# The gate product beside the sum of squares, latent norms behind counted products, and another order in the last dilated pair

## The chip, the cores and the metric

One core of a Trainium2 chip runs the whole program in one launch. The metric is the device time of one execution in microseconds (us). The kernel before took 2313.22 us, the median of three runs (2310.89 to 2314.72).

## The reference, cut to what matters

Two decoder layers over 512 positions and a model width of 1024, all in float32. Each layer is a feed-forward half step, a token mixer and a second feed-forward half step; the mixer is latent attention (MLA) in layer 0 and dilated attention in layer 1. Each of these six sub-layers sits in the same sandwich:

```python
def sandwich(x, fn, pre_g, post_g, shift, scale, gate, res_w):
    hn = rmsnorm(x, pre_g) * (1 + scale) + shift
    y = rmsnorm(fn(hn), post_g)
    return x + res_w * gate * y

def mla(h, ...):                      # the start
    lat = h @ w_in
    cq, ckv, k_rope = lat[..., :384], lat[..., 384:640], lat[..., 640:]
    q  = rmsnorm(cq,  q_norm)  @ w_q_up
    kv = rmsnorm(ckv, kv_norm) @ w_kv_up

def dilated_attention(h, ...):        # 16 heads, groups of dilation 1, 4 and 16
    o_g, lse_g = windowed attention of each group, lse_g its log of the sum of exponentials
    alpha = softmax over g of lse_g
    return (sum over g of alpha_g * o_g) @ w_o
```

## The kernel before, in words

Activations lie transposed in SBUF for the products: eight chunks `k` of 128 model columns by 512 positions, each split into a rounded part `hh` and a remainder `hl`. A float32 product is three matmuls (`mm3`, L120-126, rows L124, L125 and L126 of the trace): hi by hi, hi by lo, lo by hi. Weights come by DMA on SyncE's queue (SP) as 512 KB tiles `raw`; ScalarE (ACT) rounds them (`whi`, L107) and VectorE (DVE) forms the remainder in two halves (`wlo`, L109).

**Order of the work.** A tile scheduler orders each engine's instructions by priority. Inside `manual_schedule` an engine listed there keeps the order in which the code is written. `after(n, step)` puts off a step until `count` has seen `n` more matmul units; `mm3` counts two units for 512 columns and one for 256.

**A transition** (L390-410) goes from one sub-layer to the next. For each of four tiles of 128 positions, `tail` finishes the output product; `y_part` (L376 adds, L378 copies) brings its two halves from PSUM to SBUF, `y_done` squares them on ACT with the row sum, `scale_of` (L291 on DVE, L292 a power on GpSimd, POOL) makes the reciprocal root, `tile_done` (L413, L414) scales by root and gate and adds to the residual `x`, and `normal` (L308) makes the next normalised input. After two tiles `turn` (L418-434) transposes the pair chunk by chunk on TensorE (PE), and `modulate` applies scale and shift: for most chunks DVE makes `u` (L279), ACT rounds it to `hh` (L280) and DVE subtracts for `hl` (L281); for the chunks in `SPARE` ACT makes `hh` and `u` (L275, L276) and POOL subtracts (L277). The first products (`head`) of the next sub-layer then run over the chunks as they come. At the start of the program the same `modulate` follows a fold of the modulation weights (L158, two custom DVE instructions, each with an accumulator read, for the shift and two for the scale).

**MLA's start.** After the latents are projected, `norm` (L654-667) sums squares with narrow products (`sums`, L225), takes the root on POOL (`root`, L240 and L242), spreads it over the partitions with four products (`spread`, L248) and scales the latents, all in one call.

**The last dilated pair.** The 16 heads go in eight pairs. `scores` forms the logits, `exps` (L1058) their exponentials, `norm` (L1069-1085) the reciprocal of their sum, which goes to memory and back to change its layout (`x4` from `z0`, `d0`, then `r`), `turn` transposes the exponentials, `weigh` (L1132) multiplies them with the values, and `mix(p, step)` alternates turn and weigh. At the end `weigh` multiplies by `r` (L1142) and `put_o` hands the result to the output product. For the last pair, PE alone is ordered by hand: six `part` calls of the output product (three of its eight column blocks), then the mixes with two parts between. `part` takes one of four `mm` banks of PSUM, and the bank is free once L378 has copied it out. The last column block of `tail` needs the last pair's output.

Of the kernel before, what the change touches and what calls it, by code (L numbers as in the profile page):

```python
# [7 lines left out]
F32 = mybir.dt.float32  # L8
# [6 lines left out]
P = 128  # L15
# [14 lines left out]
SB = 4  # L30
HOT = 400
HEAD = 3
SPARE = (2, 3, 6, 7)
TURN = 26
START = 4
HT = SEQ // 2
# [16 lines left out]
class Trunk:  # L53
# [79 lines left out]
    def count(self, n):  # L133
        for d in self.due:
            d[0] -= n
        while self.due and self.due[0][0] <= 0:
            self.due.pop(0)[1]()

    def mod(self, l, n, k):
        nc = self.nc  # L140
# [169 lines left out]
    def start(self, sub):  # L310
        nc = self.nc
        mods = [(sub.l, 3 * sub.i + n) for n in (0, 1)]
        raws = {}

        def fetch(k):
            for m in mods:
                raws[m, k] = self.mod_load(*m, k)

        def fold(k):
            for m in mods:  # L320
                self.mod_halves(*m, k, raws.pop((m, k)))

        def feed(us, ks):
            for u in us:
                sub.gate_up_mm(u, 0, SEQ, banks[u], ks)

        self.first = sub
        fetch(0)
        xt = [self.bank("mm" if k < 4 else "aux") for k in range(KT)]
        with self.tc.manual_schedule(engines={ACT, DVE}):  # L330
            for i in range(TT):
                t, ss, x = [self.s(), self.s()], self.pair(), self.halves(i)
                for d in range(2):
                    self.square(x[d], t[d], ss[:, d : d + 1])
                r = self.scale_of(ss)
                for d in range(2):
                    nc.vector.tensor_scalar(t[d], x[d], r, None, ALU.mult)
                for k in range(KT):
                    nc.tensor.transpose(
                        xt[k][:, i * P : (i + 1) * P], t[k // 4][:, k % 4 * P :][:, :P], self.ident  # L340
                    )
            nc.scalar.activation(self.cs, self.cs, AF.Silu)
        self.new_h()
        units, ks = [], []
        banks = {}
        for kind, n in sorted([(n, 1) for n in range(START)] + [(n, 0) for n in range(KT)]):
            kind, n = n, kind
            if kind:
                sub.gate_up_load(n, n >= SLOTS // 2)
                banks[n] = [self.bank("mm" if 2 * n + g < 4 else "aux") for g in range(2)]  # L350
                units.append(n)
                feed((n,), ks)
                continue
            if n:
                fetch(n)
            fold(n)
            self.modulate(sub, n, 0, SEQ, xt[n], n in (3, 5, 7))
            ks.append(n)
            feed(units, (n,))
            if n == 0:  # L360
                for k in range(1, KT):
                    src, xt[k] = xt[k], self.s()
                    nc.scalar.activation(xt[k], src, AF.Copy)
        for u in units:
            sub.gate_up_out(u, 0, SEQ, banks[u])
# [16 lines left out]
    def y_done(self, i, d):  # L382
        with self.tc.high_priority(offset=HOT):
            if d == 0:
                self.ss = self.pair()
            self.square(self.y[i][d], self.t("sq", SB), self.ss[:, d : d + 1])

    def transition(self, sub, nxt):
        for u in (sub, nxt):
            if u:  # L390
                self.settle(u)
        if nxt:
            self.new_h()
        for i in range(TT):
            sub.tail(i)
            self.tile_done(nxt, i)
            if nxt and i % 2:
                self.after(TURN, lambda i=i: self.turn(nxt, i - 1))
            if nxt and i == 1:
                nxt.prepare()  # L400
        if nxt:
            for lo in (0, HT):
                for u in range(nxt.heads):
                    nxt.head(u, lo, lo + HT)
        self.count(4 * TURN)

    def tile_done(self, nxt, i):

        nc = self.nc
        r = self.scale_of(self.ss)  # L410
        for d in range(2):
            y, c = self.y[i][d], slice(d * SEQ, (d + 1) * SEQ)
            nc.vector.scalar_tensor_tensor(y, y, r, self.gb[:, c], ALU.mult, ALU.mult)  # L413
            nc.vector.tensor_tensor(self.x[:, i, c], self.x[:, i, c], y, ALU.add)  # L414
            if not nxt:
                nc.sync.dma_start(self.a["out"][i][:, c], self.x[:, i, c])
        if nxt:
            self.normal(i, self.y[i])  # L418

# [15 lines left out]

class Ffn:
    heads = HEAD

    def __init__(self, t, l, i):
        self.t, self.l, self.i, self.s = t, l, i, 0 if i == 0 else 1  # L440
# [172 lines left out]

class Mla(Mixer):
    heads = 6
    busy = False
    w_o = "mla_o"

# [35 lines left out]
    def norm(self, us, at, lo, hi):  # L654
        t, nc = self.t, self.t.nc
        n = hi - lo
        rb = t.rms([self.sq[u, lo] for u in us], n, P * len(us))
        for j, u in enumerate(us):
            if lo == 0:
                self.latn[u] = [t.s(F32R) for _ in range(2)]  # L660
            hh, hl = [x[:, lo:hi] for x in self.latn[u]]
            v = t.t("u", UB)[:, :n]
            nc.vector.scalar_tensor_tensor(
                v, self.lat[u][:, lo:hi], t.glat[:, at + j : at + j + 1], rb, ALU.mult, ALU.mult
            )
            nc.scalar.activation(hh, v, AF.Copy)
            nc.vector.tensor_tensor(hl, v, f(hh), ALU.subtract)

    def project(self, w, at, us):
        t = self.t  # L670
# [38 lines left out]
    def rope(self, g):  # L709
# [15 lines left out]


    BESIDE = {
        0: (("key", 0, 1),),
        1: (("query", 0, 1),),
        2: (("value", 2, 0),),  # L730
        3: (("value", 3, 0),),
# [92 lines left out]
    def rest(self):  # L824
        self.t.gates(self)
        self.wv, self.wqk, self.v, self.q, self.k = [], {}, {}, {}, {}
        pipe = Pipe(2)
        self.key(0, 0)
        self.rope(0)
        self.query(0, 0)  # L830
        self.value(0, 0)
        self.value(1, 0)
        for c in range(8):
            for i in range(4):
                if (c, i) == (7, 0):
                    self.t.new_y()
                self.attend(c, i, pipe)
                for name, *args in self.BESIDE.get(4 * c + i, ()):
                    getattr(self, name)(*args)
        for ns in ((3, 4, 5), (6, 7)):  # L840
            pipe.step()
            for n in ns:
                self.part(n)
        pipe.flush()


class Dil(Mixer):
    heads = 6
    busy = True
    w_o = "dil_o"  # L850
    BLOCKS = (
# [196 lines left out]
    def exps(self, p):  # L1048
        nc = self.t.nc
        pair = self.pairs[p]  # L1050
        for u, (g, blocks) in enumerate(self.BLOCKS):
            for e in range(2):
                y = pair["y"][u, e]
                at = 0
                for i, k0, n, b0 in blocks:
                    c = y[:, at : at + n]
                    one = slice(e, e + 1)
                    nc.scalar.activation(  # L1058
                        c,
                        c,  # L1060
                        AF.Exp,
                        bias=pair["top"][:, g, i, one],
                        scale=-1.0,
                        accum_out=pair["z"][:, g, i, one],
                    )
                    at += n
        self.norm(pair)

    def norm(self, pair):  # L1069
        t, nc = self.t, self.t.nc  # L1070
        z = pair["z"]
        z0 = t.dram.tile([2, SEQ, 2], F32, tag="z0", name="z0", bufs=2)
        d0 = t.dram.tile([2, SEQ], F32, tag="d0", name="d0", bufs=2)
        self.natural(z0, z)
        x = t.tmp.tile([P, 2, 4, 2], F32, tag="x4", name="x4", bufs=2)
        nc.sync.dma_start(x, z0.rearrange("g (p r) v -> p g r v", r=4))
        d = t.tmp.tile([P, 2, 4], F32, tag="w4", name="w4", bufs=2)
        dr = d.rearrange("p e r -> p r e")
        nc.vector.tensor_tensor(dr, x[:, 0], x[:, 1], ALU.add)
# [31 lines left out]
                nc.vector.tensor_copy(x[:, :n], b[:, :n])  # L1111
            out.append(x)

    def weigh(self, p, step):
        t, nc = self.t, self.t.nc
        g, _, _, products = self.TURNS[step]
        pair = self.pairs[p]
        if step == 0:
            pair["acc"] = t.bank("aux")
        v = self.qkv[p, 3 * g + 2]  # L1120
        for nth, (kt, c0, n, at) in enumerate(products):
            for e in range(2):
# [6 lines left out]
                else:  # L1129
# [3 lines left out]
                    out,  # L1133
                    v[:, kt * P + 64 * e :][:, :64],
                    rhs,
                    start=step == nth == 0,
                    stop=step == nth == 3,
                    skip_group_check=True,
                )
        if step == 3:  # L1140
            x = t.s()
            nc.vector.tensor_tensor(x, pair["acc"], pair["r"], ALU.mult)  # L1142
            self.of.append(x)
# [7 lines left out]
    def rest(self):  # L1151
# [30 lines left out]
        for x in self.of[PART:]:  # L1182
            self.put_o(x)
        self.exps(7)
        with t.tc.manual_schedule(engines={PE}):
            for n in range(6):
                self.part(n)
            for step in range(5):
                self.mix(7, step)
                if step in (1, 2):  # L1190
                    self.part(5 + step)
        self.put_o(self.of[-1])


# [113 lines left out]
```

## Time and profile before

| | |
|---|---|
| Time, median of three runs | 2313.22 us |
| The profiled execution: its own time, its span | 2314.05 us, 2312.3 us |
| Mean granted TensorE clock | 0.99 |
| PE busy | 2247.3 us, 97% of the span |
| DVE busy | 1191.8 us, 52% |
| ACT busy | 870.6 us, 38% |
| POOL busy | 121.4 us, 5% |

The span is the time from the first to the last recorded event; 1.75 us of the execution lie around it. Matmuls are pipelined, so a record of 0.39 us for a matmul of 512 columns can start 0.23 us after the one before. An idle time in brackets behind a row is the engine's own, just ahead of that row, with the instruction that ended it. The granted clock is a share of full speed (1.00 is 2.4 GHz, 0.50 is 1.2 GHz).

### The profile page before, as it was taken

To read this page: it belongs to the slowest core of one execution; us is meant where nothing else is said; L and a number is where in the kernel's file an instruction comes from. 1 tells how busy PE (TensorE), PEld (TensorE's weight loads), DVE (VectorE), ACT (ScalarE), POOL (GpSimd) and SP (SyncE) were. 2 spreads that over 40 slices of the span, in tenths; PEclk is the share of its full clock that TensorE was granted. 3 is DMA by queue.
4 is the path that set the end of the run, shared out by engine and by line. 5 is a ranking of instruction groups with operands and counts; after the bars stand their busy time and mean duration, and the time that the engine had idled before them with its cause. 6 is when DMAs were issued, how large, how long until landed. Compare 5 with 4: busy or idle time off the path is not lost. (4 is left out here: it accounts for less than half of the span.)

```text
span 2312.3 us, 30176 instructions
## 1 busy us (share of the span) xinstructions
PE 2247.3 (97%) x11418; PEld 1857.3 (80%) x11418; DVE 1191.8 (52%) x2674; ACT 870.6 (38%) x1773; POOL 121.4 (5%) x163
## 2 busy tenths in 40 slices
PE   7999999999999999999999999999999979999998
PEld 5888888877788888888888888778778758888887
DVE  7666576576655456464555453344434356233344
ACT  4422235577533222352222352443433435232232
POOL 0000001210110000020000020000000002000000
PEclk9999999999999999999999999999999989999999
DMA  8675573111345365244654423333333312242230
GB/s 311 171 241 183 171 237 104 52 56 46 105 141 182 97 205 183 81 146 124 194 171 149 123 81 100 86 86 88 94 85 83 93 38 95 74 128 91 82 110 37
DMA packets 119925, 284.55 MB, mean 123 GB/s; under 512 B 43985, under 2 KB 48356, under 8 KB 119780
## 3 DMA queue, kind: packets, MB, share of 16 engines
q1 hardware_dynamic: 119780, 282.63, 40.0%
q8 instruction: 89, 1.46, 0.3%
q14 instruction: 56, 0.46, 0.1%
HBM read 280.19 MB, written 2.39 MB: 122 GB/s over the span
## 5 line engine op out<-in xcount | busy, mean ns | idle before, releaser
L124 PE MATMUL mm<-s,whi 128*128 128x512 f32 (+1 forms) x2132 | 804.7, 379 | 10.2 <-ACT s L280 7.0
L125 PE MATMUL mm<-s,whi 128*128 128x512 f32 (+1 forms) x2132 | 800.2, 375 | 0.9 <-POOL s L277 0.7
L126 PE MATMUL mm<-s,wlo 128*128 128x512 f32 (+1 forms) x2132 | 799.1, 375 | 0.0
L107 ACT ACTIVATE whi<-raw 128x1024 fp32r<-128x1024 f32 (+1 forms) x356 | 370.2, 1053 | 989.8 <-PE mm L125 447.8
L109 DVE TENSOR_TENSOR wlo<-raw,whi 128x512 fp32r<-128x512 f32 (+1 forms) x712 | 464.9, 692 | 414.2 <-ACT whi L107 409.2
L124 PEld LDWEIGHTS mm<-s,whi 128*128 128x128 f32 x2132 | 403.6, 190 | 92.7 <-ACT s L280 8.2
L125 PEld LDWEIGHTS mm<-s,whi 128*128 128x128 f32 x2132 | 403.9, 189 | 71.7 <-POOL s L277 2.1
L126 PEld LDWEIGHTS mm<-s,wlo 128*128 128x128 f32 x2132 | 403.8, 189 | 71.2
L124 PE MATMUL mm<-whi,s 128*128 128x512 f32 x848 | 333.4, 393 | 17.1 <-DVE s L378 16.4
L125 PE MATMUL mm<-wlo,s 128*128 128x512 f32 x848 | 331.1, 390 | 0.0
L126 PE MATMUL mm<-whi,s 128*128 128x512 f32 x848 | 330.9, 390 | 0.0
L143 DVE CUSTOM_DVE_ANT_0 raw<-raw,cs 128x1024 f32<-128x1024 f32 x128 | 158.0, 1238 | 115.7 <-DMA raw<-w_mod 115.3
L124 PEld LDWEIGHTS mm<-whi,s 128*128 128x128 f32 x848 | 159.8, 188 | 52.5 <-DVE s L378 16.9
L126 PEld LDWEIGHTS mm<-whi,s 128*128 128x128 f32 x848 | 159.6, 188 | 33.5 <-issue 0.2
L125 PEld LDWEIGHTS mm<-wlo,s 128*128 128x128 f32 x848 | 159.9, 189 | 32.9 <-issue 0.2
L483 DVE TENSOR_TENSOR gg<-silu,mm 128x512 f32<-128x512 f32 (+1 forms) x95 | 60.3, 636 | 172.4 <-PE mm L126 172.0
L376 DVE TENSOR_TENSOR s<-mm,s 128x512 f32<-128x512 f32 x112 | 76.7, 689 | 126.2 <-PE mm L126 126.1
L292 POOL TENSOR_TENSOR mv<-mv,mhalf 128x1 f32<-128x1 f32 x48 | 27.3, 568 | 1492.6 <-DVE mv L291 1492.6
L484 ACT ACTIVATE s<-gg 128x512 fp32r<-128x512 f32 (+1 forms) x97 | 57.4, 591 | 55.3 <-DVE gg L483 55.2
L481 ACT ACTIVATE silu<-mm 128x512 f32<-128x512 f32 (+1 forms) x95 | 51.6, 544 | 34.0 <-PE mm L126 33.7
L125 PE MATMUL mm<-s 128*128 128x256 f32 x160 | 47.6, 303 | 14.8 <-POOL s L277 13.8
L958 ACT ACTIVATE s<-mm 128x512 f32<-128x512 f32 (+3 forms) x156 | 46.3, 374 | 37.4 <-PE mm L126 37.4
(168 smaller groups left out, 1708.8 us busy)
## 6 DMA issues: line engine op xcount, KB each, us to landing
raw<-w_gu SPq DMA_DIRECT2D x176, 512.0 KB, 4.3
raw<-w_mod SPq DMA_DIRECT2D x128, 512.0 KB, 4.8
raw<-w_down SPq DMA_DIRECT2D x88, 512.0 KB, 4.5
raw<-dil_in SPq DMA_DIRECT2D x72, 512.0 KB, 3.7
s<-w_mod SPq DMA_DIRECT2D x32, 256.0 KB, 6.6
raw<-mla_o SPq DMA_DIRECT2D x8, 512.0 KB, 3.5
raw<-dil_o SPq DMA_DIRECT2D x8, 512.0 KB, 3.7
gb<-row SPq DMA_DIRECT2D x6, 512.0 KB, 5.0
```

Source lines behind the costliest of these rows:

```text
L107: self.nc.scalar.activation(hi, raw, AF.Copy)
L109: self.nc.vector.tensor_tensor(lo[:, r], raw[:, r], f(hi[:, r]), ALU.subtract)
L124: mm(out, w[0], m[0], start=first, stop=False)
L125: mm(out, w[0], m[1], start=False, stop=False)
L126: mm(out, w[1], m[0], start=False, stop=last)
L143: nc.vector.tensor_tensor_reduce(raw, raw, self.cs, 1.0, 0.0, ALU.mult, ALU.add, accum_out=t[:, 0:1])
L292: nc.gpsimd.tensor_tensor(v[:, 1:2], v[:, 0:1], self.mhalf[:, 0:1], ALU.pow)
L376: nc.vector.tensor_tensor(y, b, y, ALU.add)
L481: nc.scalar.activation(s, banks[0], AF.Silu)
L483: nc.vector.tensor_tensor(v, s, banks[1], ALU.mult)
L484: nc.scalar.activation(ghi, v, AF.Copy)
L958: nc.scalar.activation(out, src, AF.Copy)
```

## The change

There are five parts. The gate is multiplied into `y` in `y_done`, behind the square that reads it, and `tile_done` then scales by the root and adds to `x` in one instruction. `SPARE` loses chunks 6 and 7. The fold and `modulate` of chunk 0 at the program's start move into the block in which ACT and DVE are ordered by hand. MLA's `norm` becomes two steps that are put off by 4 and by 5 counted units, and two value products and a second key product are called ahead of the rope. In the last dilated pair, `norm` splits into `norm` (sums to memory and back) and `norm_out` (adds, reciprocal, the way to `r`); DVE is ordered by hand beside PE, the mixes go in the order 2, 0, 1, 3, and `norm_out` is called behind the copies.

```diff
-SPARE = (2, 3, 6, 7)
+SPARE = (2, 3)
     def count(self, n):
         for d in self.due:
             d[0] -= n
-        while self.due and self.due[0][0] <= 0:
-            self.due.pop(0)[1]()
+        for d in [d for d in self.due if d[0] <= 0]:
+            self.due.remove(d)
+            d[1]()
...
             nc.scalar.activation(self.cs, self.cs, AF.Silu)
-        self.new_h()
+            self.new_h()
+            fold(0)
+            self.modulate(sub, 0, 0, SEQ, xt[0])
...
-            self.square(self.y[i][d], self.t("sq", SB), self.ss[:, d : d + 1])
+            y = self.y[i][d]
+            self.square(y, self.t("sq", SB), self.ss[:, d : d + 1])
+            self.nc.vector.tensor_tensor(y, y, self.gb[:, d * SEQ : (d + 1) * SEQ], ALU.mult)
...
-        self.count(4 * TURN)
+        self.count(4 * TURN if not nxt or not nxt.late else 0)
...
-            y, c = self.y[i][d], slice(d * SEQ, (d + 1) * SEQ)
-            nc.vector.scalar_tensor_tensor(y, y, r, self.gb[:, c], ALU.mult, ALU.mult)
-            nc.vector.tensor_tensor(self.x[:, i, c], self.x[:, i, c], y, ALU.add)
+            c = slice(d * SEQ, (d + 1) * SEQ)
+            x = self.x[:, i, c]
+            nc.vector.scalar_tensor_tensor(x, self.y[i][d], r, x, ALU.mult, ALU.add)
...
     def norm(self, us, at, lo, hi):                          # Mla
-        rb = t.rms([self.sq[u, lo] for u in us], n, P * len(us))
+        def total():
+            r = t.root(t.sums([self.sq[u, lo] for u in us], n), n, P * len(us))
+            t.after(5, lambda: apply(r))
+
+        def apply(r):
+            rb = t.spread(r, n)
...
+        t.after(4, total)
...
     BESIDE = {
-        0: (("key", 0, 1),),
...
         self.key(0, 0)
+        self.value(0, 0)
+        self.value(1, 0)
+        self.key(0, 1)
+        self.t.count(99)
         self.rope(0)
         self.query(0, 0)
-        self.value(0, 0)
-        self.value(1, 0)
...
         self.norm(pair)                                      # Dil.exps
+        if p < 7:
+            self.norm_out(pair)
...
-        if step == 0:                                        # Dil.weigh, now with first, last
+        if step == first:
             pair["acc"] = t.bank("aux")
...
         self.exps(7)
-        with t.tc.manual_schedule(engines={PE}):
+        order = (2, 0, 1, 3)
+        with t.tc.manual_schedule(engines={PE, DVE}):
             for n in range(6):
                 self.part(n)
-            for step in range(5):
-                self.mix(7, step)
-                if step in (1, 2):
-                    self.part(5 + step)
+            for n, step in enumerate(order):
+                self.turn(7, step)
+                if n:
+                    self.weigh(7, order[n - 1], order[0], order[-1])
+                if n in (0, 1):
+                    self.part(6 + n)
+            self.norm_out(self.pairs[7])
+            self.weigh(7, order[-1], order[0], order[-1])
```

On DVE at the last dilated pair, before: `y4` is made from the tops of the logits, `w4` is the sum and reciprocal of the last pair, the `mm` rows are the copies of the parts, `silu` and `gg` the transposed exponentials.

```order
L1039 TENSOR_TENSOR y4_15949<-y4_15949,dm_15760 128x8 [waits DVE_49]
L1079 TENSOR_TENSOR w4_16007<-x4_16005 128x4x2 [waits DMAHW0_49]
L1080 TENSOR_TENSOR w4_16007<-w4_16007,dz_15761 128x4x2 [waits DVE_49,Activation_49]
L1081 RECIPROCAL w4_16007<-w4_16007 128x8 [waits DVE_49]
L378 COPY s_15861<-mm_16017 128x512 [waits PE_49]
L378 COPY s_15862<-mm_16028 128x512 [waits PE_49]
L378 COPY s_15863<-mm_16039 128x512 [waits PE_49]
L378 COPY s_15864<-mm_16050 128x512 [waits PE_49]
L378 COPY s_15865<-mm_16061 128x512 [waits PE_49]
L378 COPY s_15866<-mm_16072 128x512 [waits PE_49]
```

The same place now, down to the add that stands first above:

```order
L381 COPY s_15864<-mm_16041 128x512 [waits PE_49]
L1055 TENSOR_TENSOR y4_15949<-x4_15947 128x8 [waits DMAHW4_49]
L1056 TENSOR_TENSOR y4_15949<-y4_15949,dm_15760 128x8 [waits DVE_49]
L381 COPY s_15865<-mm_16052 128x512 [waits PE_49]
L381 COPY s_15866<-mm_16063 128x512 [waits PE_49]
...
L381 COPY s_15868<-mm_16122 128x512 [waits PE_49]
...
L1126 STREAM_TRANSPOSE gg_16151<-u_15923 128x512 [waits DVE_49,PE_49]
L109 TENSOR_TENSOR wlo_16254<-raw_16251,whi_16253 128x512 [waits Activation_49]
...
L109 TENSOR_TENSOR wlo_16583<-raw_16580,whi_16582 128x512 [waits DMAHW7_49,Activation_49]
...
L1102 TENSOR_TENSOR w4_16158<-x4_16004 128x4x2 [waits DMAHW1_49]
L1103 TENSOR_TENSOR w4_16158<-w4_16158,dz_15761 128x4x2 [waits DVE_49]
```

The add that waits for the DMA of the sums stood ahead of all eight copies; now all eight copies, the transposes and six halves of weight remainders stand ahead of it. On SP's queue, at the same place now (`z0` to `x4`, `w4` to `d0` and `d0` to `s` are the steps of the way to `r`; before, the five followed one another without a `raw` between them):

```order
L1042 DMA z0_15998<-dz_15761 32x8 [waits DMAHW7_49]
L99 DMA raw_16587<-w_gu 128x1024 [waits DMAHW0_49,DVE_49,Activation_49]
L1094 DMA x4_16004<-z0_15998 128x2x8 [waits DMAHW5_49,DMAHW6_49,DMAHW4_49,DMAHW7_49,DMAHW3_49,DMAHW1_49]
L99 DMA raw_16704<-w_gu 128x1024 [waits DMAHW2_49,DVE_49,Activation_49]
L99 DMA raw_16711<-w_gu 128x1024 [waits DVE_49,Activation_49]
L1105 DMA d0_16157<-w4_16158 128x2x4 [waits DVE_49]
L1108 DMA s_16163<-d0_16157 64x512 [waits DMAHW4_49,PE_49]
```

Three weight loads now stand between the steps of that way. On DVE at the program's start, now (`mt` is a folded sum, `mA` and `mS` scale and shift, `u` the modulated chunk 0); before, the four custom instructions stood ahead of the first `wlo`, and `u` ahead of its last half:

```order
L159 ISA s_96,mt_202<-s_96,cs_77 128x512 [waits DMAHW7_49]
...
L109 TENSOR_TENSOR wlo_233<-raw_230,whi_232 128x512 [waits DMAHW2_49,Activation_49]
L174 SCALAR_TENSOR_TENSOR mS_91<-mt_202,small_79 128x1 [waits DMAHW5_49,DVE_49]
L159 ISA s_99,mt_206<-s_99,cs_77 128x512 [waits DMAHW0_49]
...
L159 ISA s_100,mt_206<-s_100,cs_77 128x512 [waits DMAHW1_49]
...
L109 TENSOR_TENSOR wlo_240<-raw_237,whi_239 128x512 [waits DMAHW3_49,Activation_49]
L189 SCALAR_TENSOR_TENSOR mA_90<-mt_206,small_79 128x1 [waits DVE_49]
L109 TENSOR_TENSOR wlo_240<-raw_237,whi_239 128x512
L280 TENSOR_SCALAR u_211<-mm_103,mA_90,mS_91 128x512 [waits DVE_49,PE_49]
```

A `wlo` that waits for ACT's rounding has come between the second and the third custom instruction, and all four halves of `wlo` now precede `u`.

## Rows read from the trace of the kernel before

**Rows 1.** The page, part 1: busy time, share of the span, instructions.

```profile
PE 2247.3 (97%) x11418; PEld 1857.3 (80%) x11418; DVE 1191.8 (52%) x2674; ACT 870.6 (38%) x1773; POOL 121.4 (5%) x163
```

**Rows 2.** Waits of PE: total us, times, longest us.

```profile
PE mm L124 <- DVE s L378: 16.4, 1, 16.4
PE mm L125 <- POOL s L277: 14.5, 13, 2.2
PE aux L248 <- POOL rs L242: 2.6, 4, 1.2
```

**Rows 3.** Timeline of PE, last dilated pair (start, us, what, idle before).

```profile
1871.12 0.39 PE L126 MATMUL mm<-whi,s 128*128 128x512 f32 x1
1887.95 0.79 PE L124 MATMUL mm<-whi,s 128*128 128x512 f32 x1 [16.44 <-DVE s L378]
...
1891.96 0.46 PE L124 MATMUL mm<-whi,s 128*128 128x512 f32 x1
...
1918.91 0.39 PE L126 MATMUL mm<-whi,s 128*128 128x512 f32 x1
```

**Rows 4.** Timeline of DVE, last dilated pair.

```profile
1886.65 0.17 DVE L1079 TENSOR_TENSOR w<-x 128x8 f32<-128x8 f32 x1 [14.84 <-DMA x<-z]
...
1887.26 2.43 DVE L378 COPY s<-mm 128x512 f32<-128x512 f32 x4
```

**Rows 5.** Timeline of ACT: the last exponential of the first two score blocks.

```profile
1878.46 0.49 ACT L1058 ACTIVATE sq<-sq,y 128x256 f32<-128x256 f32 x1
```

**Rows 6.** Timeline of SP's queue, last dilated pair.

```profile
1884.91 0.38 SPq L1076 DMA_DIRECT2D x<-z  x1
1887.37 0.38 SPq L1082 DMA_DIRECT2D d<-w  x1
1889.36 1.09 SPq L1085 DMA_DIRECT2D s<-d  x2
```

**Rows 7.** DMA issues from 1880 to 1900 us: KB each, median us to landing.

```profile
s<-d SPq DMA_DIRECT2D x2, 128.0 KB, 2.9
```

**Rows 8.** Timeline of POOL, from layer 0's last sub-layer into layer 1.

```profile
987.42 0.74 POOL L277 TENSOR_TENSOR s<-u,s 128x256 fp32r<-128x256 f32 x1 [3.30 <-ACT u L276]
...
993.30 4.33 POOL L277 TENSOR_TENSOR s<-u,s 128x256 fp32r<-128x256 f32 x2 [2.27 <-ACT u L276]
```

**Rows 9.** Timeline of PE, same transition.

```profile
990.05 0.39 PE L125 MATMUL mm<-s 128*128 128x256 f32 x1 [0.52 <-POOL s L277]
...
996.47 0.39 PE L125 MATMUL mm<-s 128*128 128x256 f32 x1 [2.20 <-POOL s L277]
```

**Rows 10.** Timeline of DVE, same transition.

```profile
987.98 0.99 DVE L279 TENSOR_SCALAR u<-aux,mA,mS 128x256 f32<-128x256 f32 x2
...
990.54 0.41 DVE L281 TENSOR_TENSOR s<-u,s 128x256 fp32r<-128x256 f32 x1
```

**Rows 11.** Windows of 2 us: span, busy of PE, PEld, DVE, ACT, POOL, PE's clock, DMA.

```profile
442.00:444.00 2.00, 2.00 (x6) 1.57 (x5) 0.65 (x2) 0.10 (x1) 0.00 (x0) 0.50 0.03 8
...
998.00:1000.00 2.00, 2.00 (x11) 2.00 (x11) 1.83 (x4) 1.11 (x2) 0.14 (x1) 0.50 0.64 252
```

**Rows 12.** Timeline of PE, MLA's start.

```profile
441.36 1.19 PE L124 MATMUL mm<-s,whi 128*128 128x512 f32 x2 [1.02 <-ACT s L666]
```

**Rows 13.** Timeline of all engines, end of the program.

```profile
2305.84 0.55 POOL L292 TENSOR_TENSOR mv<-mv,mhalf 128x1 f32<-128x1 f32 x1 [7.61 <-DVE mv L291]
...
2307.75 1.29 DVE L414 TENSOR_TENSOR x<-x,s 128x512 f32<-128x512 f32 x2
```

**Rows 14.** Timeline of DVE and PE, start of the program.

```profile
13.71 0.69 DVE L158 CUSTOM_DVE_ANT_0 s<-s,cs 128x512 f32<-128x512 f32 x1
...
15.94 0.69 DVE L109 TENSOR_TENSOR wlo<-raw,whi 128x512 fp32r<-128x512 f32 x1 [0.80 <-ACT whi L107]
...
17.96 0.81 DVE L279 TENSOR_SCALAR u<-mm,mA,mS 128x512 f32<-128x512 f32 x1
...
19.48 0.79 PE L124 MATMUL mm<-s,whi 128*128 128x512 f32 x1 [6.45 <-ACT s L280]
```

More of the change, by code (lines that the diff above doesn't have):

```diff
@@ L355, in start @@
                 fetch(n)
-            fold(n)
-            self.modulate(sub, n, 0, SEQ, xt[n], n in (3, 5, 7))
+                fold(n)
+                self.modulate(sub, n, 0, SEQ, xt[n], n in (3, 5, 7))
             ks.append(n)
@@ L411, in tile_done @@
         for d in range(2):
-            y, c = self.y[i][d], slice(d * SEQ, (d + 1) * SEQ)
-            nc.vector.scalar_tensor_tensor(y, y, r, self.gb[:, c], ALU.mult, ALU.mult)
-            nc.vector.tensor_tensor(self.x[:, i, c], self.x[:, i, c], y, ALU.add)
+            c = slice(d * SEQ, (d + 1) * SEQ)
+            x = self.x[:, i, c]
+            nc.vector.scalar_tensor_tensor(x, self.y[i][d], r, x, ALU.mult, ALU.add)
             if not nxt:
-                nc.sync.dma_start(self.a["out"][i][:, c], self.x[:, i, c])
+                nc.sync.dma_start(self.a["out"][i][:, c], x)
         if nxt:
@@ L437 @@
     heads = HEAD
+    late = False
     def __init__(self, t, l, i):
@@ L615 @@
     heads = 6
+    late = True
     busy = False
@@ L656, in norm @@
         n = hi - lo
-        rb = t.rms([self.sq[u, lo] for u in us], n, P * len(us))
[L658 to L667, printed above, removed]
+        def total():
[3 more added lines that the diff above has]
+            rb = t.spread(r, n)
+            for j, u in enumerate(us):
+                if lo == 0:
+                    self.latn[u] = [t.s(F32R) for _ in range(2)]
+                hh, hl = [x[:, lo:hi] for x in self.latn[u]]
+                v = t.t("u", UB)[:, :n]
+                nc.vector.scalar_tensor_tensor(
+                    v, self.lat[u][:, lo:hi], t.glat[:, at + j : at + j + 1], rb, ALU.mult, ALU.mult
+                )
+                nc.scalar.activation(hh, v, AF.Copy)
+                nc.vector.tensor_tensor(hl, v, f(hh), ALU.subtract)
+        t.after(4, total)
     def project(self, w, at, us):
@@ L848 @@
     heads = 6
+    late = False
     busy = True
@@ L1072, in norm, with norm_out @@
         z0 = t.dram.tile([2, SEQ, 2], F32, tag="z0", name="z0", bufs=2)
+        self.natural(z0, z)
+        x = pair["x"] = t.tmp.tile([P, 2, 4, 2], F32, tag="x4", name="x4", bufs=2)
+        nc.sync.dma_start(x, z0.rearrange("g (p r) v -> p g r v", r=4))
+    def norm_out(self, pair):
+        t, nc = self.t, self.t.nc
+        x, z = pair["x"], pair["z"]
         d0 = t.dram.tile([2, SEQ], F32, tag="d0", name="d0", bufs=2)
-        self.natural(z0, z)
-        x = t.tmp.tile([P, 2, 4, 2], F32, tag="x4", name="x4", bufs=2)
-        nc.sync.dma_start(x, z0.rearrange("g (p r) v -> p g r v", r=4))
         d = t.tmp.tile([P, 2, 4], F32, tag="w4", name="w4", bufs=2)
@@ L1112, in turn, with weigh @@
             out.append(x)
-    def weigh(self, p, step):
+    def weigh(self, p, step, first=0, last=3):
         t, nc = self.t, self.t.nc
@@ L1135, in weigh @@
                     rhs,
-                    start=step == nth == 0,
-                    stop=step == nth == 3,
+                    start=step == first and nth == 0,
+                    stop=step == last and nth == 3,
                     skip_group_check=True,
                 )
-        if step == 3:
+        if step == last:
             x = t.s()
```

## The prediction

> **What bounds the kernel now.** I read the page's busy times first: PE is at work in 2247.3 of 2312.3 us [rows 1], so 65 us is all that can go without taking matmuls away, and the change takes none away. The second view is the list of what PE waits for [rows 2]: one wait of 16.4 us for the copies of the last dilated pair, 14.5 us in thirteen waits for POOL's subtraction in `modulate`, 2.6 us in four waits for the root of MLA's latent norm. Third come the timelines around these waits, which say what the releaser was itself waiting for, and last the windows of the granted clock: behind a wait the matmuls run at 0.50 for a while [rows 11], so a wait costs more than its length. Each part of the change aims at one of these places, and each is priced there.
>
> **The last pair.** PE issues the last matmul of the fourth part at 1871.12 and the next only at 1887.95, 16.44 us idle [rows 3]. Its bank is freed by a copy on DVE, and DVE sat for 14.84 us on the add of the sums, which waited for a DMA [rows 4]. The nine matmuls behind the wait take 1887.95 to 1891.96, 4.01 us [rows 3], against nine times 0.227 (the spacing further on), 2.04. So 16.44 + 1.97 = 18.4 us can go at most. In the new order the copies stand ahead of that add, and none of them waits for a DMA, except that the fifth is behind the `y4` adds, whose DMA has landed by 1871.4 on the old path too. I take the wait as gone and ask what is late next.
>
> First the exponentials. The two `y4` adds now stand behind the fourth copy, so they end some 0.8 us later, and the exponentials of the first two blocks with them: 1878.46 + 0.49 [rows 5] becomes 1879.8. From 1871.35 PE has 18 matmuls (4.1), the transposes of group 1 (1.0) and nine more (2.05) to do, and reaches the next transposes at 1878.5: it waits 1.3.
>
> Then `r`. From the nine matmuls to the end of the first two tails PE works from 1891.96 to 1919.14 [rows 3], 27.2 us with nothing waiting that counts; with the nine at full clock 29.2, of which the last 12 matmuls (2.7) need the last pair's output. PE can start them at 1871.35 + 26.5 + 1.3 = 1899.2. The way to `r`: the load of `x4` used to go at 1884.91 [rows 6]. Now a weight load stands ahead of it on SP's queue, which waits until DVE has worked off a `wlo` behind the last copies. I place those at 1886.1, two halves of `wlo` (0.6 each at the pace of rows 14) at 1887.3, the issue of `x4` at 1887.7. The add could start 1.74 later as it did before (1884.91 to 1886.65 [rows 4, 6]), at 1889.4, but two stream transposes and four more halves stand ahead of it on DVE: 1.3 + 2.5, so about 1891.1. Sum and reciprocal take 0.6, from the issue of `d` to that of `s` 2.0 passes [rows 6], the second `s` and its landing take another 1.1 + 2.9 [rows 6, 7]: `r` is there near 1897.7. The product with `acc` (0.69) and ACT's rounding (0.63) bring it to 1899.0, beside PE's 1899.2. I take 0.5 us of wait. **Term: 18.4 - 1.3 - 0.5 = 16.6 us less**; bounds 18.4, and 12 if the weight loads ahead of `x4` and `d` make `r` 5 us later.
>
> **SPARE.** POOL's subtraction of 256 columns takes 0.74 us alone, but two took 4.33 when DVE was full of subtractions [rows 8]; PE then waited 0.52 and 2.20 [rows 9], and these two waits stand alike at the three transitions out of a feed-forward, 2.72 each. Chunks 6 and 7 now cost DVE 0.5 for `u` and 0.4 for `hl` each [rows 10], 1.8 in all for a half, and their `hl` no longer stands behind two POOL instructions. Walking the new order of DVE and ACT at 990 us, I find the wait at chunk 2 still there and about half a microsecond at chunk 7: 1.0 where 2.72 was. Where the long wait dropped the clock, 14 matmuls ran 0.21 apart and not 0.12, another 1.3 us; that was so at two of the three. Together 3 x 1.7 + 2 x 1.3 = 7.7. At the transition out of MLA, where most of the remaining 6.3 us of rows 2 stands with the one out of dilated attention, DVE is busy too: I take 2. **Term: 9.7 less**, bounds 4 and 16.
>
> **Out of dilated attention.** Here the first part bunches the work. Tiles 0 and 1 used to end one after the other; now their last 12 matmuls come together, at about 1899.5 to 1902.2, and DVE has the adds, gate products, roots and scalings of both in a row. At 0.7 each I get tile 1 normalised at 16.3 us behind the first of these matmuls, where PE, with 30 matmuls of tile 2 and 24 of tile 3, comes to its transposes at about 15; and the `hl` of chunk 0 comes some 2.7 us after PE could use it. These waits, about 5 us in all, take the place of some 4.5 there now (half of that 6.3, and the 1.3 for the clock). **Term: 0.5 more**, bounds 2.5 less and 4 more.
>
> **Latent norms.** The four waits for the root, 2.6 us [rows 2], the wait of 1.02 for the scaled latents [rows 12] and the slow clock behind it (0.50 from 442 to 444 [rows 11]; some seven matmuls 0.2 us late each) make 5.1. The root now has five counted products of cover before it is spread, 1.1 us of 512-column products or more, against 0.7 on POOL and an add on DVE ahead of it. I keep about 1 for waits that reappear when value and key products need the last scaled latent. **Term: 4 less**, bounds 6 less and 0.
>
> **Gate product.** It exchanges two instructions per half for two; DVE is not what PE waits for there, so only the end of the program gains. Behind the last power came two scalings and then the adds, 1.29 us for the pair [rows 13]; now the gate is multiplied in during the power, and one instruction per half is left. **Term: 1.2 less**, bounds 1.4 and 0.
>
> Beside the long pair of POOL instructions in rows 8 stood DVE instructions with two SBUF operands. The Trainium skill, page "SBUF — State Buffer", section "SBUF: two separate sides", says why that may be: DVE and POOL share a port pair as an exclusive lock, and the one that comes second waits out the other's instruction. By this rule the second gate product, which now starts just ahead of the last power, holds that power back by up to its own 0.69 us, and the end gains 0.6 and not 1.2; by rows 13, where the power ran beside nothing, it gains 1.2. I keep 1.2 in the sum; by the rule the time would be 0.6 later.
>
> **Start.** `u` of chunk 0 started at 17.96, PE at 19.48 [rows 14]. Now the first half of `wlo`, which waits for ACT until 15.94, stands ahead of the third and fourth custom instruction (0.6 each, 13.71 [rows 14]), and all four halves ahead of `u`: 16.55 + 1.25 + 3 x 0.6 + small ones 0.2 = 19.8 to 19.9. The whole chain on ACT and DVE moves with it, and PE has nothing else. **Term: 2.0 more**, bounds 0 and 2.2.
>
> **Sum.** -16.6 - 9.7 + 0.5 - 4 - 1.2 + 2.0 = -29.0. The profiled execution took 2314.05 us, 0.8 above the median of 2313.22; 2314.05 - 29.0 = 2285.
>
> **Rivals.**
> - *The stall only moves.* PE waits for `r`, since SP's queue and DVE both put weight work ahead of its way. For: three loads and six `wlo` halves are now in it. Against: 26 us of PE work lie before it. With `r` 5 us late and the clock dropping as it did at 1888 (2 us): 2285 + 7 = 2292.
> - *DVE takes POOL's place in the transitions.* 3.6 us more work for the two halves falls in the stretch where DVE also makes weight remainders and normalises tiles. Then the 9.7 are not gained: 2295. For: with four `u` buffers, `u` of chunks 6 and 7 waits for POOL to finish with chunks 2 and 3. Against: POOL's first two took 0.74 alone.
> - *Slower than before.* The same mechanism, stronger: in both halves of all five transitions PE waits for the `hl` of chunks 6 and 7 behind weight remainders. Per half 1.8 of added work, two halves of `wlo` (1.2) and 1.3 for the clock, 4.3 in all, ten times: 2295 + 43 = 2338. It decides from a wait of 1.9 us a half on, 19 us over all. Against: in the second halves PE has the first half's products of several heads to go on with.
> - *It does not do what it says.* A copy still stands behind something that waits for memory, and the last pair gains less than half: 2285 + 9 = 2294. The new DVE order speaks against it.
>
> **How the numbers follow.** Forecast 0.5, stall moves 0.17, DVE in POOL's place 0.18, copies stuck 0.05, the first two rivals together (2302) 0.06, slower 0.04. The forecast's own bounds, with two or three terms off at once, give about 2277 to 2293; the next cases reach 2302, so the range is 2275 to 2302. A measurement of this kernel tells 0.2% (4.6 us) from no change. Half of the 2302 case may run past 2308.6, which gives the 0.03 of no change: faster 0.93, no change 0.03, slower 0.04.
>
> **What would show it.** No PE wait over 2 us between 1863 and 1900, and the sum behind the copies; PE's waits for POOL's subtraction down from thirteen and 14.5 us to under 8, with no wait above 1.3 out of a feed-forward; no wait for the root in MLA's start; the first weighted matmul near 21.5; the last output DMA 1.2 us sooner behind the last matmul. Wrong would be a wait for the rounded last block, for `hl` on DVE at three or more transitions, or a clock at 0.50 behind any of them.

## The result, and where the time went

The changed kernel takes 2278.47 us (median of four runs, 2275.93 to 2279.77) against 2312.05 for the kernel before: ratio 0.9854, 95% interval 0.9837 to 0.9871, some 34 us less. The forecast was 2285 within 2275 to 2302.

The profiled spans are 2278.0 and 2312.3 us, 34.3 us apart. To see where, I read when PE issues the same matmul in both traces: the first and last 256-column product of each transition, the last scores of MLA, the first and last scores of the dilated attention, the last matmul. The difference between two such points is what lies between them:

| Stretch | Forecast | Measured |
|---|---|---|
| Start, up to the first transition | +2.0 | +1.55 |
| Five transitions: T1 FFN to MLA, T2 MLA to FFN, T3 FFN to FFN, T4 FFN to dilated, T5 dilated to FFN | -9.2 | -1.70, -4.90, -3.84, -3.83, -4.09: -18.4 |
| MLA, up to its last scores | -4 | -0.49 |
| Dilated attention, first to last scores | 0 | -0.51 |
| Last pair and tails | -16.6 | -15.44 |
| End, behind the last matmul | -1.2 | -0.95 |
| The rest (feed-forwards, MLA behind its scores) | 0 | -0.1 |

Two terms were far off, the transitions by 9.2 us and MLA by 3.5, in opposite directions. First the list of PE's waits after (us in total, times, longest), against [rows 2]:

```profile
PE mm L783 <- ACT s L739: 2.0, 1, 2.0
...
PE mm L124 <- ACT s L614: 1.1, 1, 1.1
...
PE mm L125 <- DVE s L282: 1.1, 4, 0.5
PE aux L249 <- POOL rs L243: 0.9, 1, 0.9
...
PE mm L125 <- POOL s L278: 0.8, 2, 0.4
PE mm L783 <- ACT s L722: 0.8, 1, 0.8
```

The wait of 16.4 us is gone, POOL's fourteen and a half are 0.8, three of the four waits for the root are gone, and the first of them, 0.45 before, is now 0.9. New are 2.0 and 0.8 us ahead of MLA's first scores (L783) and 1.1 for the rounded last block (L614). In the last pair, DVE's timeline answers to [rows 4]:

```profile
1857.76 0.69 DVE L381 COPY s<-mm 128x512 f32<-128x512 f32 x1 [1.27 <-PE mm L126]
1858.36 0.16 DVE L1055 TENSOR_TENSOR y<-x 128x8 f32<-128x8 f32 x1
...
1875.98 0.17 DVE L1102 TENSOR_TENSOR w<-x 128x8 f32<-128x8 f32 x1 [0.35 <-DMA x<-z]
...
1884.46 0.69 DVE L1165 TENSOR_TENSOR s<-aux,s 128x512 f32<-128x512 f32 x1 [7.86 <-DMA s<-d]
```

The copies wait only for PE. The add comes when its DMA does, 0.35 us later than DVE is ready for it, and what is late is `r`: DVE idles 7.86 us for it. SP's queue, as in [rows 6], shows why:

```profile
1872.10 0.36 SPq L99 DMA_DIRECT2D raw<-w_gu  x1
1872.68 0.86 SPq L1094 DMA_DIRECT2D x<-z  x1
1874.49 1.55 SPq L99 DMA_DIRECT2D raw<-w_gu  x2
1876.63 0.38 SPq L1105 DMA_DIRECT2D d<-w  x1
1880.95 1.09 SPq L1108 DMA_DIRECT2D s<-d  x2
```

From `x4`'s issue to the add it takes 3.3 us where it took 1.74, from `d` to `s` 4.3 where it took 2.0. The end of the program, against [rows 13]:

```profile
2272.19 0.16 DVE L292 SCALAR_TENSOR_TENSOR mv<-ss 128x1 f32<-128x1 f32 x1 [0.85 <-ACT sq L285]
2272.26 0.69 DVE L391 TENSOR_TENSOR s<-s,gb 128x512 f32<-128x512 f32 x1
2272.49 0.86 POOL L293 TENSOR_TENSOR mv<-mv,mhalf 128x1 f32<-128x1 f32 x1 [7.29 <-DVE mv L292]
2273.39 1.41 DVE L419 SCALAR_TENSOR_TENSOR x<-s,mv,x 128x512 f32<-128x512 f32 x2 [0.44 <-POOL mv L293]
```

The gate product lies beside the power, which takes 0.86 us and not 0.55 [rows 13].

Stretches that an experiment leaves alone still differ from execution to execution: T1 takes 1.7 or 3.0 us less than before, MLA up to its scores 0.4 to 0.5 or 2.1, the dilated attention 0.5 to 0.9 or 2.4 to 3.0. In T1 and MLA the two values go with the granted clock. PE's waits there (0.95, 2.00 and 0.78 us) are the same in this trace and in that of `p_act` below; behind them the clock is at 0.50 from 404 to 406 and from 452 to 454 us here, and at 1.00 throughout there. In the dilated attention PE waits 0.93 and 0.33 us for exponentials near 1695 us in this trace, and not in `p_act` or `q_hoist`. T2 to T4 repeat within 0.03 us. So the experiments are read from these points and not from single times. Of the kernel before there is one profile. In it the clock is at 0.50 behind POOL's waits at T3 and T4 (1.3 us each in my forecast); whether that is so in its other executions is not known.

### The profile page after: what moved, and what is told of

Same layout as the page of the kernel before. It is cut to its first block, busy times and chain, and to the rows that moved or that the text cites. A ratio compares the mean times of both kernels' runs of the same rounds, so it can differ in the third digit from the quotient of the medians.

```text
span 2278.0 us, 30160 instructions
## 1 busy us (share of the span) xinstructions
PE 2241.2 (98%) x11418; PEld 1854.1 (81%) x11418; DVE 1205.5 (53%) x2714; ACT 862.6 (38%) x1753; POOL 104.7 (5%) x143
## 3 DMA queue, kind: packets, MB, share of 16 engines
HBM read 280.19 MB, written 2.39 MB: 124 GB/s over the span
## 5 line engine op out<-in xcount | busy, mean ns | idle before, releaser
L293 POOL TENSOR_TENSOR mv<-mv,mhalf 128x1 f32<-128x1 f32 x48 | 36.0, 751 | 1492.6 <-DVE mv L292 1490.1
L383 ACT ACTIVATE s<-mm 128x512 f32<-128x512 f32 x40 | 23.8, 595 | 86.0 <-PE mm L126 85.7
```

Source lines behind the costliest of these rows:

```text
L293: nc.gpsimd.tensor_tensor(v[:, 1:2], v[:, 0:1], self.mhalf[:, 0:1], ALU.pow)
```

## The experiments

**Undoing one part of the transitions.**

```diff
-SPARE = (2, 3)                 # u_spare: only this
+SPARE = (2, 3, 6, 7)
```

> The changed kernel with SPARE back at (2, 3, 6, 7). Theory A, the subtractions on POOL are what PE waited for in all five transitions: the 18.4 us that the transitions lost come back almost whole, thirteen waits for L278 of some 14 us in all and the half clock behind the long ones; time 2294 to 2297. Rival B, the gate product moved ahead of the root shortens the chain to the normalised tile and gave half of it: only about 9 us come back, time 2287, and PE waits for POOL under 8 us.

2281.7 us (median of four runs, ratio to before 0.9868, interval 0.9854 to 0.9883): 3 us more than the changed kernel, not 18. T2 to T5 lose 3.95, 3.62, 3.52 and 3.31 us against before even with POOL's four subtractions a half. Theory A falls; it is nearer to B and beyond it.

```diff
-            self.nc.vector.tensor_tensor(y, y, self.gb[...], ALU.mult)          # u_gate: y_done
...
-            nc.vector.scalar_tensor_tensor(x, self.y[i][d], r, x, ALU.mult, ALU.add)
+            nc.vector.scalar_tensor_tensor(y, y, r, self.gb[:, c], ALU.mult, ALU.mult)
+            nc.vector.tensor_tensor(self.x[:, i, c], self.x[:, i, c], y, ALU.add)
```

> The changed kernel with the gate multiplied in behind the root again, two instructions per half in tile_done. Theory A: the transitions don't move (each within 0.5 us), the end of the program is 1 us longer, time 2279 to 2280; the mean of POOL's power falls from 751 ns back to about 570, as no product with two operands in SBUF stands beside it. Rival B: the transitions take 9 us more, time 2287.

2286.19 us (median of four runs, 0.9888, 0.9872 to 0.9905), B's time. T2 to T5 lose only 2.40, 2.68, 3.40 and 2.40, and the last pair with its tails 12.3 where it lost 15.4. T1 goes the other way: it loses 4.5, more than the 1.7 or 3.0 of the changed kernel. The end is 0.9 us longer and the power is back at 599 ns, so that part of A holds. PE's timeline of this kernel at T3 shows the new wait, at the transposes of the second turn:

```profile
991.86 0.55 PE L430 MATMUL aux<-ident,s 128*128 128x128 f32 x3 [1.08 <-ACT s L308]
```

L308 is the normalised tile: with two instructions a half behind the root it comes 1.08 us too late. So I formed another theory: either part alone removes POOL's long waits, and the gate part also brings the normalised tile sooner. Each part alone on the kernel before, `gate_alone` and `spare_alone`, tests it:

> The kernel before with one part of the change alone, the gate product ahead of the root. Theory A, this part by itself takes away the long waits for POOL, since fewer DVE instructions follow the root while POOL subtracts: the transitions out of the feed-forwards and out of MLA lose 3.3 to 4 us each, as in the kernel that lacks only the SPARE edit, with the end of the program 14 to 17 us in all, 2296 to 2299. Rival B, it worked only together with the other parts: under 6 us.

> The kernel before with SPARE = (2, 3) alone. Theory A, as in the kernel that lacks only the gate part: 2.4 to 3.4 us less at each of the later transitions, about 10 to 13 us in all, with the wait for the normalised tile in the second turn that the old scaling leaves; 2300 to 2303. Rival B, my forecast's 9.7 us in all and no wait for the normalised tile: 2304.

2297.56 us (median of four runs, 0.9949, 0.9932 to 0.9966) and 2300.05 (one run). The kernel before took 2308.72 beside them, so they are 11.2 and 8.7 us faster: the gate part's absolute time fits theory A, its gain falls short of the 14 to 17 us. In the profiles the spans are 16.3 and 14.0 us shorter, because the one profile of the kernel before is of an execution of 2314.05. The three transitions that no other part of the change touches:

| Against before, us | T2 | T3 | T4 | Sum |
|---|---|---|---|---|
| SPARE alone | -2.39 | -2.67 | -3.41 | -8.5 |
| Gate product alone | -3.94 | -3.62 | -3.52 | -11.1 |
| Both (the change) | -4.90 | -3.84 | -3.83 | -12.6 |
| Both, and no chunk on POOL (below) | -5.26 | -4.17 | -4.16 | -13.6 |

The parts overlap: 8.5 + 11.1 would be 19.6, the two give 12.6. At T5 SPARE alone loses 1.6 us and the gate product alone 4.3. At T1 SPARE alone loses 2.7, but the gate product alone takes 1.16 us more, against theory A, which had it lose 3.3 to 4 there too. PE reaches the squares of the latents sooner and waits for them, and the clock is at 0.54 behind it (404 to 406 us):

```profile
401.24 0.61 PE L225 MATMUL aux<-ones,sq 128*128 128x1 f32 x4 [1.56 <-ACT sq L259]
```

How the gate part frees POOL stands in POOL's timeline of that kernel at T3, with four chunks in SPARE:

```profile
988.21 0.73 POOL L277 TENSOR_TENSOR s<-u,s 128x256 fp32r<-128x256 f32 x1
989.87 0.88 POOL L277 TENSOR_TENSOR s<-u,s 128x256 fp32r<-128x256 f32 x1 [0.93 <-ACT u L276]
```

These are chunks 6 and 7, which took 4.33 us for two [rows 8] and now take 0.73 and 0.88. DVE still works beside them, but it has just been idle for 0.44 us, waiting for the power, and POOL's first subtraction starts 0.06 us ahead of DVE's next instruction:

```profile
988.27 1.88 DVE L416 SCALAR_TENSOR_TENSOR x<-s,mv,x 128x512 f32<-128x512 f32 x2 [0.44 <-POOL mv L292]
```

Now DVE's rows are the longer ones: 1.88 us for two scalings that take 1.41 at the program's end, where POOL is idle. In the kernel before, DVE ran without a gap from 991.7 to 997.0 us, so POOL's subtractions began while it was at work.

**Does DVE become the bound?** On the best version so far (below), SPARE is emptied.

```diff
-SPARE = (2, 3)                  # best_none
+SPARE = ()
```

> The same with SPARE empty, so POOL has no subtraction in the transitions and DVE makes u and hl of all eight chunks. Theory A, DVE is full there and becomes the bound: PE waits for DVE's L282 at four or five transitions, 2 to 5 us more than with chunks 2 and 3 on ACT and POOL. Rival B, POOL is still what PE waits for, since DVE's instructions stretch its own: the waits of 0.4 us go and the time is 1 to 2 us less.

2269.92 us (median of four runs, 0.9827, 0.9811 to 0.9843), 3 us less than with chunks 2 and 3 on POOL. Theory A falls, and with it my rival that DVE takes POOL's place. Of rival B's 1 to 2 us, 1.0 shows at T2 to T4; T5 takes 0.65 more. T1 takes 2.2 less in the two profiles, but some 1.3 of that is the clock, at 0.50 there in the execution with chunks 2 and 3 on POOL and at 1.00 in this one, so the whole 3 us is not shown to be the edit's. PE does wait for DVE more often, but briefly:

```profile
PE mm L125 <- DVE s L282: 3.5, 10, 0.5
```

**MLA's start.**

```diff
-        t.after(4, total)                  # u_latent: root and spread at once, as before
...
-        self.value(0, 0)
-        self.value(1, 0)
-        self.key(0, 1)
-        self.t.count(99)
         self.rope(0)
         self.query(0, 0)
+        self.value(0, 0)
+        self.value(1, 0)
```

> The changed kernel with MLA's norm, its order of products and the count at the transition's end as before. Theory A, the wait only moved from the root to the rope: the waits for the root (2.6 us) and for the scaled latent (1.0) and the slow clock behind come back, the waits for the rope's copies (2.0 and 0.8) and the slow clock behind them go; from the transition's last 256-column matmul to MLA's last scores it takes 0.5 us more. Rival B, the counted products gave the 4 us that I had forecast and something else took 3.5: 4 us more there.

One run, 2280.42. From T1's end to MLA's last scores it takes what it took before, 0.49 us more than in the changed kernel, and the waits come and go as theory A says. The 0.49 holds for executions with the slow clock behind the new waits; in `p_act` and `p_sums`, where the clock stays at 1.00, the new order gains 2.1 there and another 1.3 in T1. In the changed kernel PE's timeline reads

```profile
449.13 0.49 PE L783 MATMUL mm<-s 96*128 96x128 f32 x2 [2.00 <-ACT s L739]
450.40 1.35 PE L783 MATMUL mm<-s 96*128 96x128 f32 x6 [0.78 <-ACT s L722]
```

and the window behind it has the clock at 0.50, as 442 to 444 had before [rows 11]:

```profile
452.00:454.00 2.00, 2.00 (x6) 1.55 (x5) 0.83 (x5) 1.82 (x9) 0.00 (x0) 0.50 0.00 0
```

The value products that used to lie between the rope and the first scores now lie ahead of the rope. Another product in that place:

```diff
-        1: (("query", 0, 1),),          # q_hoist: BESIDE
...
         self.query(0, 0)
+        self.query(0, 1)
```

> The changed kernel with MLA's second query product (9 matmuls, 2.05 us) called right behind the first instead of beside the second attention step. Theory A, PE waits 2.0 and 0.8 us there because the rope's way over DVE, POOL and ACT takes 4.2 us and only one query product lies beside it: the first wait is gone, the second below 0.3, and the matmuls behind stay at full clock; up to MLA's last scores 2 to 4 us less. Rival B, the product is only missing later, beside the softmax of the second step: 0 to 1 us less.

One run, 2272.75; up to MLA's last scores 4.00 us less than before, 3.5 less than the changed kernel's profile and 1.9 less than the best value of that stretch. The wait of 2.0 is gone, the clock behind is at 1.00, and the wait of 0.8 for L722 stays. Theory A, but for that wait; 1.9 is the gain with the clock at 1.00 in both.

**The start.**

```diff
-            self.new_h()                   # u_start: out of the block ordered by hand
-            fold(0)
-            self.modulate(sub, 0, 0, SEQ, xt[0])
+        self.new_h()
...
-                fold(n)
-                self.modulate(sub, n, 0, SEQ, xt[n], n in (3, 5, 7))
+            fold(n)
+            self.modulate(sub, n, 0, SEQ, xt[n], n in (3, 5, 7))
```

> The changed kernel with the fold and modulate of chunk 0 outside the block ordered by hand, as before. Theory A, the half of the weight remainder between the custom instructions is what delays the start: the first 512-column matmul at 19.4 to 19.6 instead of 21.4, and the 1.9 us stay to the end. Rival B, the start is held by the DMA of the weights and the delay is absorbed by the next waits: at the first transition under 0.5 us are left of it.

One run, 2274.57. Theory A: the first matmul comes at

```profile
19.39 0.80 PE L124 MATMUL mm<-s,whi 128*128 128x512 f32 x1 [6.24 <-ACT s L281]
```

and at the first transition PE stands 0.06 us ahead of before, where the changed kernel is 1.55 behind. The run takes fold and `modulate` out of the hand order as a whole; which of the `wlo` halves ahead of `u` costs what, it does not separate.

**The last pair.**

```diff
-        if p < 7:
-            self.norm_out(pair)
+        self.norm_out(pair)                # p_sums; the later call is dropped
```

> The changed kernel with the last pair's adds and reciprocal issued with the sums again, ahead of the copies; the order 2, 0, 1, 3 and DVE's order by hand stay. Theory A, the place of these adds alone made the stall: PE idles 15 to 17 us for L381 in the last pair, and from the first part to the first 256-column matmul of the next sub-layer it takes 14 to 16 us more. Rival B, the order of the mixes carries part: at most half of that, 8 us.

One run, 2290.49. The stall is back whole:

```profile
1869.06 0.79 PE L124 MATMUL mm<-whi,s 128*128 128x512 f32 x1 [16.30 <-DVE s L381]
```

Last pair and tails take 0.66 us more than before instead of 15.44 less: theory A, the place of the adds makes it all.

```diff
-        order = (2, 0, 1, 3)               # p_order
+        order = (0, 1, 2, 3)
```

> The changed kernel with the last pair's mixes in the order 0, 1, 2, 3. Theory A, group 1 first matters since its exponentials are the first that ACT finishes: PE waits about 3 us for the exponentials of the first blocks ahead of the transposes, of which the wait for r behind takes back 1: 2 us more from the first part to the next sub-layer. Rival B, the place of the adds alone counts: within 0.5 us.

One run, 2281.17. PE waits 2.3 us for exponentials, of which the wait for `r` gives back 0.7; the last pair loses 13.4 where it lost 15.4. Theory A by the size of 2.0; T5 loses another 0.8 less.

```diff
-            self.norm_out(self.pairs[7])   # p_act: and so for x4 in norm
+            self.norm_out(self.pairs[7], t.nc.scalar)
```

> The changed kernel with the last pair's way to r (x4, d0 and the two loads of r) issued by ACT instead of SP, so no weight load stands ahead of it in its queue. Theory A, the queue's order is what makes r late: x4 is issued 1.5 us earlier, r lands 2 to 4 us earlier and PE's wait of 1.14 us for the rounded last block goes; 1 us less up to the next sub-layer. Rival B, the loads' traffic slows these small transfers in whatever queue they are: from d to s again over 4 us, and the wait stays above 0.7.

One run, 2277.56. The way to `r` on ACT's queue:

```profile
1867.76 0.41 ACTq L1094 DMA_DIRECT2D x<-z  x1
1872.21 0.37 ACTq L1105 DMA_DIRECT2D d<-w  x1
1876.61 1.14 ACTq L1108 DMA_DIRECT2D s<-d  x2
```

From `d` to `s` it is 4.4 us again, and PE waits 1.4; the last pair and T5 together lose 2.1 us less than in the changed kernel. Rival B: these small transfers are slow while 512 KB loads run, whichever of the two queues issues them. I had put it down to the order on SP's queue. No run held the loads back alone, but `p_sums` comes near it: there the adds come early, no load is under way at this step (the DMA moves about 2 GB/s, against some 200 in the changed kernel), and from `d` to `s` it is 1.92 us.

**The best version.** The change with the start as before and the second query product hoisted.

> The changed kernel with the two edits that paid in single runs: the start as before (1.9 to 2.0 us less) and the second query product behind the first (2 to 3.5 us less). The places are 400 us apart and independent, so they add: 4 to 5.5 us less than the changed kernel, 2273 to 2275. Rival: the weights' traffic moves with the start and one of the two is lost, 2276 or more.

2272.94 us (median of five runs, 0.9837, 0.9821 to 0.9853). Against the changed kernel's profile MLA gives 3.5 us and the start 0.9 and not 1.6 to 2.0, since the first matmul still comes 0.76 us later than before: 4.4 in all, inside the 4 to 5.5. With SPARE empty it is the 2269.92 above, the fastest kernel of the study: 1.7% less than before, against 1.5% for the change.

## Why the prediction was right, and which steps were not

- **The last pair: right.** 16.6 forecast, 15.4 measured, and the add's place is shown to be the cause. Inside it, the wait for the exponentials that I priced at 1.3 us did not come, since the `y4` adds were ready for their data; the wait for `r` was 1.14 and not 0.5. The step that failed is the 2.0 us "from the issue of `d` to that of `s`", taken over from a stretch in which no weight load ran: it measured 4.3.
- **"DVE is not what PE waits for there, so only the end of the program gains": wrong.** This step of the gate product is the largest miss. Alone it takes 11.1 us off T2 to T4 and 4.3 off T5, where SPARE alone takes 8.5 and 1.6; only at T1 it gains nothing. I had counted instructions (two for two) and not where they stand: one of two now precedes the root, so the normalised tile and the residual come one instruction a half sooner, and POOL's subtractions start in the gap in which DVE waits for the root. That this gap is what shortens them is read from the rows; no run changed it by itself.
- **SPARE: right in mechanism, term 9.7.** Alone it gives 8.5 at T2 to T4 and 2.7 at T1, 11.2 over the four transitions of the term. Of the wait of 1.0 us that I left at each transition out of a feed-forward, the 0.5 at chunk 2 is there with SPARE alone; the half microsecond at chunk 7 is not, and in its place PE waits 1.08 us at T3 and 0.20 at T4 for the normalised tile. In the change 0.6 remains, 0.42 for ACT's rounding and 0.2 for `hl` on DVE.
- **Out of dilated attention: wrong sign.** I forecast 0.5 more and T5 lost 4.1. The bunching is there as small waits, 0.4 us for the normalised tile and 0.5 for `hl`, but the 2.7 us for chunk 0 did not come: with the gate product still behind the root that very place waits 2.95 us for L281. I had walked DVE's rows without their shorter chain behind the root.
- **Latent norms: too much.** Three of the four waits for the root went, the first one is 0.95 us now, and 2.0 and 0.8 came ahead of the first scores: the cover was taken from the rope. "I keep about 1 for waits that reappear" should have been the rope's 4.2 us of DVE, POOL and ACT less one query product, 2.05, with the clock behind. Three of the root's waits lie inside T1, so T1 and MLA count together: against the one trace of `u_latent` the part gives 0.5 us in the changed kernel's profile, with the clock at 0.50 behind two of the new waits, and 3.4 in `p_act` and `p_sums`, with the same waits and the clock at 1.00. The forecast was 4.
- **Start and end: right.** First matmul at 21.37 for a forecast of 21.5, 1.55 kept of 2.0; end 0.95 for 1.2. The page "SBUF — State Buffer" of the Trainium skill (section "SBUF: two separate sides") has DVE and POOL wait out each other's instruction on a shared port; by it the end would have gained 0.6. The trace agrees in direction: the power beside the product takes 0.86 us, in the kernel without that product 0.55. The product had 0.46 us left when the power started (2272.49 to 2272.95), so 0.31 of 0.46 is lost, and not the whole 0.69.
- **Signs of being wrong.** Two that I had named came, both small: the 1.14 us for the rounded last block, and `hl` on DVE at four transitions, 0.5 us at most. The clock is at 1.00 behind them.
- **The sum: partly luck.** The misses add up to 5.3 us in the profiles because the transitions' extra 9.2 and the latent norms' missing 3.5 have opposite signs, and the larger one comes from an effect that the forecast had denied.

## What to carry to other kernels

Behind a reduction that others wait for, count the instructions between its result and the consumer, not the instructions in all: moving one ahead of the root was worth more than the engine change that was aimed at the wait (left out of the change, they cost 7.7 and 3.2 us). Before products are moved to cover one wait, look for the wait that they cover now. And two edits that aim at the same wait don't add; leave each one out, and try each alone, before crediting either.

## What the runs showed of the hardware that I had not expected

From the issue of a 4 KB write to memory (`d`) to the issue of the loads that wait for it, 4.3 to 4.4 us passed with two or three 512 KB loads under way, on SP's queue and on ACT's (changed kernel, `p_act`). On SP's queue without such loads it was 1.99 and 1.92 (kernel before, `p_sums`).

The same waits of PE, 0.95, 2.00 and 0.78 us, were followed by a granted clock of 0.50 in one execution (changed kernel) and by 1.00 in others (`p_act`, `p_sums`), which is worth 1.3 us at T1 and 1.6 in MLA. A gain of that size is to be checked against the clock before an edit is credited with it.

And emptying SPARE, which gives DVE the subtractions of all chunks, was not slower although DVE is the busier engine: PE's waits for its `hl` are ten of at most 0.5 us, and the clock stays at 1.00 from 600 to 660 us, over all of T2.
